# Head projection weights split one projection ahead, and the final norm's products divided by rows between GpSimd and VectorE

## The chip, the core and the metric

The kernel runs on one core of one Trainium2 chip. The metric is device time in microseconds (us). A core has TensorE (PE, the matrix engine, with its weight loads listed as PEld), VectorE (DVE), ScalarE (ACT), GpSimd (POOL) and SyncE (SP), which here only issues DMA transfers. Each engine works through its own queue in order; an instruction whose operand is not ready holds all that stand behind it on that engine. Engines wait for each other by semaphores.

## What is computed

Three different transformer blocks run one after the other on one sequence of 512 tokens with 1024 features, all in float32. The change touches the end of block 1 and the middle of block 3. Block 1 ends with its residual sum and a final norm, and block 2 begins with a norm of its own:

```python
x = x + g2 * expert_choice_ffn(hx2, w_router[l], w_gate[l], w_up[l], w_down[l])
return rms_norm(x, norm_final)          # block 1
...
h = rmsnorm(x, pre_mix_g)               # block 2, first line
```

Block 3 has a mixer with two branches that start from one product of the normed input with `w_in`: latent attention with 8 heads, and a convolution over 31 tokens with a layer norm behind it. Cut to what the change touches:

```python
c_q, c_kv, k_r, u_glu, gate_logits = jnp.split(h @ w_in, IN_OFFSETS, axis=-1)
q = (rms_norm_3(c_q, q_norm) @ w_uq)    # 8 heads x (128 nope + 64 rope columns)
k_nope = rms_norm_3(c_kv, kv_norm) @ w_uk    # 8 heads x 128
scores = q_nope @ k_nope + rope(q_rope) @ rope(k_r)     # then causal softmax, @ v
u = layer_norm(conv31(u_a * sigmoid(u_b)))   # then silu, @ w_pw2
```

## The kernel before

A float32 product is done as three products of two halves: an operand `a` is split into `ah` (a rounded copy, cast by ScalarE at L470) and `al` (the rest, `a - ah`, by VectorE or GpSimd at L471), and TensorE sums `ah*bh`, `ah*bl` and `al*bh` into one PSUM bank. Both operands are split, weights too: `w` gives `wh` and `wl`.

The code is written as generators, one for each strand of work. `run` takes a step of the strand whose made-up clock is behind the others; the numbers in `yield` are what a step is supposed to last. That and a scheduler of the framework fix the order of every engine's queue when the program is built; nothing is decided on the chip.

Head stage of block 3. Five strands run together. `fill3` gives TensorE the bulk of its work: first the rest of the products of `w_in` with the normed input (tiles h3h, h3l, results pj and then gt), then, as soon as the convolution's result uh is there, the 8 blocks of `w_pw3` with it (uhh, uhl). `conv_ln` does the last convolution rows on VectorE (L2207, cv), sums columns on TensorE (cs), subtracts the mean (L2414), squares on ScalarE (L2419, ucq), sums again, scales (L2430, L2438), and ends with a tanh (th), a product on VectorE (L2441, uc) and the split into uhh (ScalarE, L2443) and uhl (GpSimd, L2444). `projs` makes the heads' operands by `proj`, and `heads` does the attention of two heads at a time in `head_pair`: scores (at), softmax on VectorE and ScalarE (mx, prob), transposes of the probabilities on TensorE (pT, copied as probT), and products with v (ao).

`proj(hd)` loads, for every even head, the weights of two heads from `w_uq` into one tile wq (384 columns for the rope parts of both, then 384 for each nope part), makes qr (rope part of the pair), qn (nope part of the head) and kn (from the tile wm, `w_uk`). Each of these three projections goes through `small`: split the weight into wsh and wsl, yield 1600, then 9 products (6 for kn) into the bank sp. The text calls them r1, n2, k2 and so on: r with the number of the pair, n and k with that of the head. There are 4 + 8 + 8 = 20 such splits. The weights of `w_in`, `w_pw3` and so on (tile w) are split on ScalarE and GpSimd. All loads and stores of this stage, wq, w and the stores of gt to memory, stand in SP's one queue; the tiles wq, wm and w share four buffers.

End of block 1. `fin_row(t)` takes the four 128-token rows t = 0 to 3 as four strands. For each it adds the last expert's output to the residual (L1346), multiplies its two halves j = 0, 1 of 512 columns by the gain (L1421, tile y), sums the squares of x and of y on ScalarE (L646, junk), raises to the power -0.5 on GpSimd (L605), scales (L1438, xs) and transposes on TensorE for block 2 (L675, tr, and the split h2h, h2l). The products of L1421 run on VectorE for j = 0 and on GpSimd for j = 1.

Of the kernel before, what the change touches and what calls it, by code (L numbers as in the profile page):

```python
# [11 lines left out]
F32 = mybir.dt.float32  # L12
# [4 lines left out]
OP = mybir.AluOpType  # L17
# [296 lines left out]
def kernel(ctx: ExitStack, tc: tile.TileContext, A, out):  # L314
    nc = tc.nc
    V, P, SC, PE = nc.vector, nc.gpsimd, nc.scalar, nc.tensor

    glob = ctx.enter_context(tc.tile_pool(name="glob", bufs=1))
    wraw = ctx.enter_context(tc.tile_pool(name="wraw", bufs=4))
# [4 lines left out]
    def T(name, dt=F32, n=512):  # L324
        return heap.tile([128, n], dt, name=name, tag="t")
# [6 lines left out]
    def SM(name, n, dt=F32):  # L332
        assert n <= 32
        return glob.tile([128, n], dt, name=name, tag="sm", bufs=24)

    def PS(name="ps"):
        return psum.tile([128, 512], F32, name=name, tag="ps")
# [27 lines left out]
    def tok(t):  # L365
        return slice(128 * t, 128 * t + 128)
# [100 lines left out]
    def split(src, name, w=512, eng=None):  # L467
        hi = T(name + "h", F32R, w)
        lo = T(name + "l", F32R, w)
        SC.copy(hi, src)  # L470
        (eng or V).tensor_tensor(lo, src, hi.bitcast(F32), op=OP.subtract)  # L471
        return hi, lo

    def flat(name, sizes, unit=None):

        off = 0
        for n in sizes:
            yield (A[name][off:off + 128 * n].rearrange("(p c) -> p c", p=128), n,
                   None if unit is None else [unit] * (n // unit), name, None)
            off += 128 * n  # L480
# [35 lines left out]
    for g in G3:  # L516
        n = (b + g + 1) // 2 - (b + 1) // 2
# [3 lines left out]
    ws = Stream(main, [4, 4])  # L521
# [7 lines left out]
    def mm3(ps, a, b, start, stop):  # L529
        mm(ps, a[0], b[0], start, False)  # L530
        mm(ps, a[0], b[1], False, False)
        mm(ps, a[1], b[0], False, stop)
# [71 lines left out]
    def pow_half(y, m, n):  # L604
        P.tensor_tensor(y, m, mhalf[:, :n], op=OP.pow)  # L605
# [28 lines left out]
    def rows_b(name, o=0, w=512):  # L634

        a = T(name)
        src = A["rows"]
        nc.sync.dma_start(a[:, :w], bass.AP(tensor=src.tensor, offset=src.offset + _ROFF[name] + o,
                                            ap=[[0, 128], [1, w]]))
        return a  # L640

    def mean_sq(row):

        ss = SM("ss", 2)
        for j in range(2):
            SC.activation(junk, row[j], AF.Square, scale=1.0 / 32, accum_out=ss[:, j:j + 1])  # L646
        return ss

    def rstd(ss, eps=EPS):
        m = SM("m", 1)  # L650
        V.scalar_tensor_tensor(m, ss[:, 0:1], eps, ss[:, 1:2], op0=OP.add, op1=OP.add)  # L651
        r = SM("r", 1)
        pow_half(r, m, 1)
        return r
# [15 lines left out]
    def turn(t, xs, h):  # L670

        for j in range(2):
            ps = PS("tr")
            for c in range(4):
                PE.transpose(ps[:, tok(c)], xs[j][:, tok(c)], ident)  # L675
            hk, lk = h.h[j][:, :, tok(t)], h.l[j][:, :, tok(t)]
            SC.copy(hk, v4(ps))  # L677
            yield 800
            V.tensor_tensor(lk, v4(ps), hk.bitcast(F32), op=OP.subtract)  # L679
        yield 800  # L680
# [7 lines left out]
    def load_rows(ap, nt, name):  # L688
        r = []
        for t in range(nt):  # L690
            r.append([T(name), T(name)])
            for j in range(2):
                nc.sync.dma_start(r[t][j], ap[tok(t), 512 * j:512 * j + 512])
        return r
# [89 lines left out]
    for k in range(KD):  # L784
# [4 lines left out]
        h, l = hx(k)  # L789
# [101 lines left out]
    for o in range(0, _NM, 512):  # L891
        a = T("mf")
        w = min(512, _NM - o)
# [257 lines left out]
    x1 = load_rows(A["x"], TT, "x1")  # L1151
# [187 lines left out]
    def combine_row(e, t):  # L1339
        ygh, ygl = yg[e]  # L1340
        for d in range(2):
            pc = PS("pc")
            r = slice(64 * d, 64 * d + 64)
            mm(pc, sct[e][r, tok(t)], ygh[r], True, False)
            mm(pc, sct[e][r, tok(t)], ygl[r], False, True)
            V.tensor_tensor(x1[t][d], x1[t][d], pc, op=OP.add)  # L1346
# [6 lines left out]
    for e in range(NE):  # L1353
        hT = [None, None]
        if e == NE - 1:
            ws.caps = [4, 4]
            nf = [rows_b("norm_final", 512 * j) for j in range(2)]
# [29 lines left out]
        for q in range(8):  # L1387
            w, rel = ws.raw()
            for kk in range(2):
                f = 2 * q + kk  # L1390
                p, c, j = f // 8, (f // 4) % 2, f % 4
# [9 lines left out]
        a = T("yg")  # L1401
# [11 lines left out]
    def fin_row(t):  # L1413

        yield 1000 * t
        combine_row(NE - 1, t)
        yield 1500
        y = []
        for j in range(2):
            a = T("y")  # L1420
            (P if j else V).tensor_tensor(a, x1[t][j], nf[j], op=OP.mult)  # L1421
            y.append(a)
        ss = mean_sq(x1[t])
        yield 1700
        r = rstd(ss)
        s2 = mean_sq(y)
        yield 1500
        m, q, r2 = SM("m", 1), SM("q", 1), SM("r2", 1)
        V.tensor_tensor(m, s2[:, 0:1], s2[:, 1:2], op=OP.add)
        V.tensor_tensor(q, r, r, op=OP.mult)  # L1430
        V.tensor_scalar(m, m, q, EPS, op0=OP.mult, op1=OP.add)
        pow_half(r2, m, 1)
        V.tensor_tensor(r2, r2, r, op=OP.mult)
        yield 1200
        xs = []
        for j in range(2):
            a = T("xs")
            V.scalar_tensor_tensor(a, y[j], r2, gm[j], op0=OP.mult, op1=OP.mult)  # L1438
            xs.append(a)
            yield 700  # L1440
        xbs[t] = y, r
        yield from turn(t, xs, h2)
        turned.add(t)
# [98 lines left out]

    proj2 = Persist(dense_t(ws, range(11), h2, use_rw, lead=LD[0]))
    run(*[fin_row(t) for t in range(TT)], proj2.steps(LD[0], lambda: len(turned) > 1))
    del x1, nf, gm
    table("sigmoid_and_others")
# [7 lines left out]
    src = A["rows"]  # L1554
# [719 lines left out]
    cq, ck = pair(cqp), pair(ckp)  # L2274

    def rope(a, dst):
        pr = PS("rot")
        mm(pr, con("rot"), a, True, True)
        b = T("ropeb")
        P.tensor_tensor(dst, a, rope_t[1], op=OP.mult)  # L2280
        V.tensor_tensor(b, pr, rope_t[0], op=OP.mult)
        P.tensor_tensor(dst, dst, b, op=OP.add)
# [5 lines left out]
    uk = list(flat("w_uk3", [2048], 256))  # L2288
    uq = list(flat("w_uq3", [1152] * 4, 384))
    mla_specs += uk + uq  # L2290
    ml = {}
# [9 lines left out]
    def mla_pre():  # L2301

        while 5 not in lat:
            yield 1000
        mla_loads()
        yield from latent_norm([lat[3], lat[4]], 256, "kv_norm_3", "ckn", ckp)
        yield from latent_norm([lat[0], lat[1], lat[2]], 384, "q_norm_3", "cqn", cqp)
        kr = lat[5]
        rope(kr, kr)
        yield 4000  # L2310
        us = []
        for j in range(4):
            us.append(split(ml["uv"][:, 512 * j:512 * j + 512], "wv"))
            yield 1300
        for j in range(2):
            for t in range(TT):
                ps = PS("v3")
                for k in range(2):
                    mm3(ps, ck(k, tok(t)), us[2 * j + k], k == 0, k == 1)
                SC.copy(v3[t][j], ps)  # L2320
                yield 1300
        del ml["uv"]
        for hd in range(2):
            yield from proj(hd)

    def small(src, kd, h):
        u = split(src, "ws", 128 * kd)
        yield 1600
        ps = PS("sp")
        for k in range(kd):  # L2330
            mm3(ps, (u[0][:, tok(k)], u[1][:, tok(k)]), h(k), k == 0, k == kd - 1)
        return ps

    def proj(hd):
        p, h = divmod(hd, 2)
        if h == 0:
            w = wraw.tile([128, 2048], F32, name="wq", tag="w")
            nc.sync.dma_start(w[:, :1152], uq[p][0])
            ml["q"] = w
            yield 4000  # L2340
            qr = T("qr")
            SC.copy(qr, (yield from small(w[:, :384], 3, cq)))
            yield 2500
            ql = T("qro")
            rope(qr, ql)
            ml["qr"] = ql
            yield 2000
        qn = T("qn")
        SC.copy(qn, (yield from small(ml["q"][:, 384 + 384 * h:768 + 384 * h], 3, cq)))
        yield 2500  # L2350
        kn = T("kn3")
        V.tensor_copy(kn, (yield from small(ml["uk"][:, 256 * hd:256 * hd + 256], 2, ck)))
        yield 2000
        qk[hd] = qn, kn, ml["qr"]

# [25 lines left out]
    def projs():  # L2381
        while not pre.over:
            yield 500
        for hd in range(2, 8):
            while hd > done[0] + 3:
                yield 1000
            yield from proj(hd)
# [144 lines left out]
```

## Time and profile before

| | us |
|---|---|
| median of 3 runs | 3052.68 (3047.94 to 3056.89) |
| the profiled execution | 3049.72 |
| its span in the trace | 3047.9 |
| TensorE busy in it | 2790.1 (92%) |
| VectorE busy | 1278.3 (42%) |
| ScalarE busy | 788.0 (26%) |
| GpSimd busy | 463.0 (15%) |

Block 1's mixer and experts last to about 1400 us of the span, block 2 from there to about 2170, block 3 from there to the end; the head stage of block 3 lies between about 2355 and 2595. A line of the timeline gives start and duration in us, engine, line, operation, output and inputs, shape and count; in brackets stands the idle time of the engine just before, and what ended it. Products on TensorE overlap, so their spacing is read from the starts.

### The profile page before, as it was taken

The numbers are of one execution on the slowest core, as the hardware profiler recorded it, in microseconds if no ns is written. First come the engines' busy times: TensorE is split into PE (matmuls) and PEld (weight loads), VectorE is DVE, ScalarE is ACT, GpSimd is POOL, SyncE is SP. The second block draws the span as 40 slices with busy tenths as digits, with TensorE's granted clock in tenths as the row PEclk, the third lists the DMA queues.
The fourth block names the chain that finished last, engine by engine and source line by source line (L and its number), as shares of the span: only waits on it lengthen the run. The fifth ranks groups of instructions, "written<-read, shape, count | busy, mean of one in ns | idle before, by whom it ended". The sixth has DMA issues, their size and how long they took to land.

```text
span 3047.9 us, 34789 instructions
## 1 busy us (share of the span) xinstructions
PE 2790.1 (92%) x13924; PEld 1865.3 (61%) x13924; DVE 1278.3 (42%) x2362; ACT 788.0 (26%) x1629; POOL 463.0 (15%) x438
## 2 busy tenths in 40 slices
PE   6989879898899898886998999999998989999999
PEld 4866564242233232224776788888886756788887
DVE  4157652112111111114377753333699654543334
ACT  3233220000000000004233333223433343442322
POOL 1034230000000000001320111010254332210100
PEclk8999989999999999998999999999999999999999
DMA  6233547999999999996110222222322212422221
GB/s 265 69 118 119 200 172 289 425 425 425 425 425 425 425 426 425 425 423 246 56 42 1 74 93 97 104 83 104 115 97 98 74 60 99 150 84 105 103 90 62
DMA packets 83041, 605.25 MB, mean 199 GB/s; under 512 B 9216, under 2 KB 9472, under 8 KB 29376
## 3 DMA queue, kind: packets, MB, share of 16 engines
q1 hardware_dynamic: 82800, 602.78, 50.0%
q8 instruction: 109, 1.79, 0.2%
q14 instruction: 52, 0.43, 0.0%
q0 software_dynamic: 80, 0.26, 0.0%
HBM read 592.52 MB, written 10.49 MB: 198 GB/s over the span
## 4 chain that ended last, share of the span: by engine, by line
PE 65%; DMA 18%; DVE 12%; ACT 2%; issue 2%; POOL 1%; SPq 0%; DVEq 0%; POOLq 0%; ACTq 0%
PE pj L527 25%; PE pn L527 15%; PE pg L527 9%; DMA wb<-in_w_down_dram 5%; DMA wb<-in_w_gate_dram 4%; DMA wb<-in_w_up_dram 4%; DVE cv L2207 3%; PE py L527 3%; DMA w<-in_w_up_dram 2%; PE pc L527 2%; PE xs L527 1%; PE sp L527 1%; PE at L527 1%; DMA w<-in_w_gate_dram 1%; DMA w<-in_w_down_dram 1%
## 5 line engine op out<-in xcount | busy, mean ns | idle before, releaser
L471 DVE TENSOR_TENSOR wl<-w,wh 128x512 fp32r<-128x512 f32 (+1 forms) x416 | 293.8, 749 | 210.9 <-ACT wh L470 160.1
L527 PE MATMUL pg<-wb,xs 128*64 128x512 f32 x1216 | 287.8, 617 | 51.8 <-DMA wb<-in_w_up_dram 28.0
L470 ACT CAST wh<-w 128x512 fp32r<-128x512 f32 (+1 forms) x510 | 288.5, 617 | 99.2 <-PE pn L527 92.3
L527 PEld LDWEIGHTS pg<-wb,xs 128*64 128x64 f32 x1216 | 87.0, 141 | 228.9 <-issue 155.9
L605 POOL TENSOR_TENSOR r<-m,mhalf 128x1 f32<-128x1 f32 x46 | 30.8, 672 | 1191.1 <-DVE m L651 1185.6
L527 PE MATMUL pg<-w,xs 128*64 128x512 f32 x800 | 188.3, 602 | 5.6 <-DMA w<-in_w_up_dram 3.5
L527 PE MATMUL py<-wb,hidT 128*64 128x512 f32 x584 | 138.8, 622 | 37.9 <-DMA wb<-in_w_down_dram 37.9
L527 PE MATMUL pn<-wh,fh 128*128 128x512 f32 x432 | 168.1, 389 | 0.0
L527 PE MATMUL pn<-wh,fl 128*128 128x512 f32 x432 | 168.1, 389 | 0.0
L527 PE MATMUL pn<-wl,fh 128*128 128x512 f32 x432 | 168.1, 389 | 0.0
L2207 DVE SCALAR_TENSOR_TENSOR cv<-glua,vecs,cv 128x486 f32<-128x486 f32 (+27 forms) x232 | 165.3, 735 | 4.7
L471 POOL TENSOR_TENSOR wl<-w,wh 128x512 fp32r<-128x512 f32 x94 | 124.5, 1344 | 151.1 <-ACT wh L470 114.8
L527 PE MATMUL pj<-h2fh,wh 128*128 128x512 f32 (+1 forms) x376 | 141.3, 378 | 2.5 <-ACT h2fh L677 2.5
L527 PE MATMUL pj<-h2fl,wh 128*128 128x512 f32 (+1 forms) x376 | 141.8, 377 | 0.2 <-DVE h2fl L679 0.2
L527 PE MATMUL pj<-h2fh,wl 128*128 128x512 f32 (+1 forms) x376 | 141.8, 377 | 0.0
L527 PE MATMUL pj<-h3h,wh 128*128 128x512 f32 (+1 forms) x336 | 128.1, 381 | 0.9 <-ACT h3h L677 0.9
L527 PE MATMUL pj<-h3l,wh 128*128 128x512 f32 (+1 forms) x336 | 125.9, 375 | 0.5 <-DVE h3l L679 0.5
L527 PE MATMUL pj<-h3h,wl 128*128 128x512 f32 (+1 forms) x336 | 125.7, 374 | 0.0
L527 PEld LDWEIGHTS pg<-w,xs 128*64 128x64 f32 x800 | 54.5, 137 | 116.1 <-issue 91.0
L1402 DVE SCALAR_TENSOR_TENSOR yg<-py,gsl,g2h 128x512 f32<-128x512 f32 x16 | 12.0, 750 | 261.3 <-PE py L527 261.3
L527 PEld LDWEIGHTS py<-wb,hidT 128*64 128x64 f32 x584 | 43.6, 142 | 127.4 <-issue 97.7
L1334 ACT COPY hidT<-hT 128x512 f32<-128x512 f32 x32 | 18.8, 586 | 393.4 <-PE hT L1332 393.4
(613 smaller groups left out, 5675.2 us busy)
## 6 DMA issues: line engine op xcount, KB each, us to landing
wb<-in_w_gate_dram SPq DMA_DIRECT2D x40, 2048.0 KB, 20.4
wb<-in_w_down_dram SPq DMA_DIRECT2D x36, 2048.0 KB, 20.8
wb<-in_w_up_dram SPq DMA_DIRECT2D x36, 2048.0 KB, 19.7
w<-in_w_down_dram SPq DMA_DIRECT2D x54, 1024.0 KB, 20.4
w<-in_w_up_dram SPq DMA_DIRECT2D x52, 1024.0 KB, 20.0
w<-in_w_gate_dram SPq DMA_DIRECT2D x48, 1024.0 KB, 22.1
w<-in_w_in_dram SPq DMA_DIRECT2D x35, 1024.0 KB, 5.0
w<-in_w_ff_dram SPq DMA_DIRECT2D x30, 1024.0 KB, 4.8
```

The source lines that it names most:

```text
L470: SC.copy(hi, src)
L471: (eng or V).tensor_tensor(lo, src, hi.bitcast(F32), op=OP.subtract)
L527: PE.matmul(ps, a, b, start=start, stop=stop, **kw)
L605: P.tensor_tensor(y, m, mhalf[:, :n], op=OP.pow)
L1334: SC.copy(h, pt)
L1402: V.scalar_tensor_tensor(a, py, gsl[:, e:e + 1], g2h, op0=OP.mult, op1=OP.mult)
L2207: V.scalar_tensor_tensor(acc[:, sh:], a[:, :512 - sh], w[j], acc[:, sh:], op0=OP.mult, op1=OP.add)
```

## The change

`small` no longer splits its own weight at the spot. A weight can be split by `cut` beforehand, and each call of `small` issues, ahead of its own pause and products, the split of the weight that comes next (`nxt`): r names n, n names k, and k of an even head names n of the odd head; k of an odd head names none, so that r and the next pair's n are split when r's turn comes. The load of wq for the next pair moves from the beginning of that pair to the place behind the last nope part of this pair, and the pause of 4000 after it stays for the first pair alone. In `fin_row`, L1421 now runs on GpSimd for both halves of rows 0 and 1 and on VectorE for both halves of rows 2 and 3.

```diff
@@ fin_row
-            (P if j else V).tensor_tensor(a, x1[t][j], nf[j], op=OP.mult)
+            (P if t < 2 else V).tensor_tensor(a, x1[t][j], nf[j], op=OP.mult)
@@
-    def small(src, kd, h):
-        u = split(src, "ws", 128 * kd)
+    cuts = {}
+    def cut(hd, nm):
+        src, kd = {"r": (lambda: ml["q"][:, :384], 3), "n": (lambda: ml["q"][:, 384 + 384 * (hd % 2):768 + 384 * (hd % 2)], 3),
+                   "k": (lambda: ml["uk"][:, 256 * hd:256 * hd + 256], 2)}[nm]
+        cuts[hd, nm] = split(src(), "ws", 128 * kd), kd
+    def small(hd, nm, nxt, h):
+        if (hd, nm) not in cuts:
+            cut(hd, nm)
+            yield 1600
+        if nxt is not None:
+            cut(*nxt)
         yield 1600
+        u, kd = cuts.pop((hd, nm))
         ps = PS("sp")
...
+    def load_q(p):
+        w = wraw.tile([128, 2048], F32, name="wq", tag="w")
+        nc.sync.dma_start(w[:, :1152], uq[p][0])
+        ml["q"] = w
     def proj(hd):
         p, h = divmod(hd, 2)
         if h == 0:
-            w = wraw.tile([128, 2048], F32, name="wq", tag="w")
-            nc.sync.dma_start(w[:, :1152], uq[p][0])
-            ml["q"] = w
-            yield 4000
+            if p == 0:
+                load_q(0)
+                yield 4000
...
-        SC.copy(qn, (yield from small(ml["q"][:, 384 + 384 * h:768 + 384 * h], 3, cq)))
+        SC.copy(qn, (yield from small(hd, "n", (hd, "k"), cq)))
+        if h and hd < 7:
+            load_q(p + 1)
         yield 2500
         kn = T("kn3")
-        V.tensor_copy(kn, (yield from small(ml["uk"][:, 256 * hd:256 * hd + 256], 2, ck)))
+        V.tensor_copy(kn, (yield from small(hd, "k", None if h else (hd + 1, "n"), ck)))
```

Three places where this moves instructions. The first is VectorE during the softmax of head pair 0, where the split of n2 (wsl from wq) stands. Before:

```order
L2414 TENSOR_TENSOR uc<-uc,cb 128x512 x2
L2281 TENSOR_TENSOR ropeb<-rot,sinB 128x512
L1830 RECIPROCAL mx<-mx 128x1 x2
L1831 TENSOR_SCALAR prob<-prob,mx 128x512 x2
L471 TENSOR_TENSOR wsl<-wq,wsh 128x384
L1854 COPY probT<-pT 128x512
```

Now (lines behind the diff are 20 higher, so L2210 keeps its number and L2411 is L2431):

```order
L1831 TENSOR_SCALAR prob<-prob,mx 128x128
L471 TENSOR_TENSOR wsl<-wq,wsh 128x384
L2210 SCALAR_TENSOR_TENSOR uc<-glua,vecs,cv 128x512
L1831 TENSOR_SCALAR prob<-prob,mx 128x128
L1830 RECIPROCAL mx<-mx 128x1
L1831 TENSOR_SCALAR prob<-prob,mx 128x256
L2431 TENSOR_SCALAR mu<-cs_15311 128x4
```

The split went from behind the last scaled probabilities of the pair to ahead of the last convolution row (L2210).

The second is the end of the convolution's layer norm, while the softmax of head pair 1 runs, on VectorE. There wq is split for the nope parts of pair 2 and wm for k4. Before:

```order
L2281 TENSOR_TENSOR ropeb<-rot,sinB 128x512
L2441 SCALAR_TENSOR_TENSOR uc<-th,uc 128x512
L1830 RECIPROCAL mx<-mx 128x1
L1831 TENSOR_SCALAR prob<-prob,mx 128x512
L2441 SCALAR_TENSOR_TENSOR uc<-th,uc 128x512
L471 TENSOR_TENSOR wsl<-wq,wsh 128x384
L1854 COPY probT<-pT 128x512
```

Now:

```order
L1831 TENSOR_SCALAR prob<-prob,mx 128x512
L471 TENSOR_TENSOR wsl<-wm,wsh 128x256
L1830 RECIPROCAL mx<-mx 128x1
L1831 TENSOR_SCALAR prob<-prob,mx 128x512
L2461 SCALAR_TENSOR_TENSOR uc<-th,uc 128x512 x3
L471 TENSOR_TENSOR wsl<-wq,wsh 128x384
L1854 COPY probT<-pT 128x512
```

The split behind the last uc was n4's and is now n5's; n4's stands further up, and k4's ahead of the second 128x512 probability; three uc stand behind that probability instead of one. On ScalarE the same place reads, before:

```order
L470 CAST wsh<-wq 128x384
L2443 CAST uhh<-uc 128x512
L2349 COPY qn<-sp 128x512
L470 CAST wh<-w 128x512 x5
L1854 COPY probT<-pT 128x512
```

Now:

```order
L470 CAST wsh<-wq 128x384
L2463 CAST uhh<-uc 128x512
L1854 COPY probT<-pT 128x512
L470 CAST wh<-w 128x512 x5
L1854 COPY probT<-pT 128x384
```

The copy qn of n4's products went further up, and the casts of the five next weight units now stand behind the first copy of transposed probabilities instead of qn.

The third is GpSimd at the end of block 1 (x_2890 and x_2891 are the halves of row 0, x_2894 and x_2895 of row 1, x_2899 and x_2903 second halves of rows 2 and 3):

```order
 L605 TENSOR_TENSOR r<-m,mhalf 128x1
+L1421 TENSOR_TENSOR y<-x_2890,norm_final 128x512
 L1421 TENSOR_TENSOR y<-x_2891,norm_final 128x512
+L1421 TENSOR_TENSOR y<-x_2894,norm_final 128x512
 L1421 TENSOR_TENSOR y<-x_2895,norm_final 128x512
-L1421 TENSOR_TENSOR y<-x_2899,norm_final 128x512
-L1421 TENSOR_TENSOR y<-x_2903,norm_final 128x512
 L605 TENSOR_TENSOR r<-m,mhalf 128x1
```

GpSimd keeps four products at the same place in its queue, between the power for row 0 and the next one; VectorE takes the four of rows 2 and 3 instead of the first halves, with one small operation (L651) in their middle instead of behind them.

On SP the loads of wq after the first are issued earlier: the second keeps its place but for one swap of a store with a load, the third moves ahead of the first two loads of `w_pw3`, the fourth ahead of the last.

## Rows read from the trace of the kernel before

**Rows 1.** The page: busy time, share of the span, instructions of TensorE and others.

```profile
PE 2790.1 (92%) x13924; PEld 1865.3 (61%) x13924; DVE 1278.3 (42%) x2362; ACT 788.0 (26%) x1629; POOL 463.0 (15%) x438
```

**Rows 2.** TensorE's waits, 2355 to 2575 us: us in total, times, longest.

```profile
PE sp L527 <- ACT wsh L470: 12.5, 5, 6.7
PE sp L527 <- DVE wsl L471: 5.5, 2, 3.1
```

**Rows 3.** Timeline of TensorE in the head stage, rows with idle time ahead.

```profile
2397.37 0.50 PE L527 MATMUL sp<-cknh,wsh 128*128 128x512 f32 x1 [0.98 <-ACT wsh L470]
...
2431.49 0.50 PE L527 MATMUL sp<-cqnh,wsl 128*128 128x512 f32 x1 [3.10 <-DVE wsl L471]
...
2485.51 0.79 PE L527 MATMUL sp<-cqnh,wsh 128*128 128x512 f32 x1 [6.68 <-ACT wsh L470]
...
2493.62 0.79 PE L527 MATMUL pj<-uhh,wh 128*128 128x512 f32 x1 [1.19 <-ACT wh L470]
...
2517.81 0.50 PE L527 MATMUL sp<-cknh,wsh 128*128 128x512 f32 x1 [1.07 <-ACT wsh L470]
...
2588.81 1.98 PE L527 MATMUL ao<-probT,v 128*128 128x512 f32 x4 [0.77 <-ACT probT L1854]
```

**Rows 4.** Busy time by windows: stretch, length, each engine, clock, DMA.

```profile
2440.00:2464.00 24.00, 24.00 (x123) 17.84 (x121) 12.16 (x24) 7.62 (x17) 2.29 (x2) 1.00 0.25 85
2464.00:2494.00 30.00, 16.55 (x51) 8.49 (x51) 23.32 (x54) 16.58 (x39) 14.12 (x11) 0.83 0.01 5
```

**Rows 5.** Timeline of TensorE after its waits: the spacing of products.

```profile
2432.54 0.57 PE L527 MATMUL sp<-cqnh,wsh 128*128 128x512 f32 x1
...
2435.90 0.45 PE L527 MATMUL pj<-h3h,wh 128*128 128x512 f32 x1
...
2494.98 0.80 PE L527 MATMUL pj<-uhh,wl 128*128 128x512 f32 x1
...
2497.59 0.39 PE L527 MATMUL pj<-uhh,wl 128*128 128x512 f32 x1
2497.82 0.40 PE L527 MATMUL pj<-uhh,wh 128*128 128x512 f32 x1
...
2498.52 1.58 PE L1852 MATMUL pT<-cons,prob 128*128 128x128 f32 x13
```

**Rows 6.** Timelines of VectorE, ScalarE and GpSimd where uh is finished.

```profile
2485.73 1.75 DVE L2441 SCALAR_TENSOR_TENSOR uc<-th,uc 128x512 f32<-128x512 f32 x1
2487.41 1.61 DVE L471 TENSOR_TENSOR wsl<-wq,wsh 128x384 fp32r<-128x384 f32 x1
...
2487.52 0.62 ACT L2443 CAST uhh<-uc 128x512 fp32r<-128x512 f32 x1 [2.06 <-DVE uc L2441]
...
2485.49 4.67 POOL L2444 TENSOR_TENSOR uhl<-uc,uhh 128x512 fp32r<-128x512 f32 x3
2493.65 6.22 POOL L471 TENSOR_TENSOR wl<-w,wh 128x512 fp32r<-128x512 f32 x5 [3.49 <-ACT wh L470]
```

**Rows 7.** Timelines of VectorE (splits of r0, r1 and r2) and SP (second wq).

```profile
2368.28 0.76 DVE L471 TENSOR_TENSOR wsl<-wq,wsh 128x384 fp32r<-128x384 f32 x1 [4.33 <-ACT wsh L470]
...
2411.42 1.64 DVE L471 TENSOR_TENSOR wsl<-wq,wsh 128x384 fp32r<-128x384 f32 x1
...
2473.36 0.55 DVE L471 TENSOR_TENSOR wsl<-wq,wsh 128x384 fp32r<-128x384 f32 x1
...
2391.93 0.33 SPq L2338 DMA_DIRECT2D wq<-in_w_uq_dram  x1
```

**Rows 8.** Timelines of VectorE, GpSimd and TensorE at the final norm.

```profile
1407.73 4.63 DVE L1421 TENSOR_TENSOR y<-x,norm_final 128x512 f32<-128x512 f32 x4
1413.42 0.15 DVE L1429 TENSOR_TENSOR m<-ss 128x1 f32<-128x1 f32 x1
...
1408.79 5.91 POOL L1421 TENSOR_TENSOR y<-x,norm_final 128x512 f32<-128x512 f32 x4
...
1416.76 1.97 PE L675 MATMUL tr<-cons,xs 128*128 128x128 f32 x8 [12.77 <-DVE xs L1438]
```

More of the change, by code (lines that the diff above doesn't have):

```diff
@@ L2336, in proj @@
         if h == 0:
-            w = wraw.tile([128, 2048], F32, name="wq", tag="w")
-            nc.sync.dma_start(w[:, :1152], uq[p][0])
-            ml["q"] = w
-            yield 4000
+            if p == 0:
+                load_q(0)
+                yield 4000
             qr = T("qr")
-            SC.copy(qr, (yield from small(w[:, :384], 3, cq)))
+            SC.copy(qr, (yield from small(hd, "r", (hd, "n"), cq)))
             yield 2500
```

## The prediction

> **What bounds the kernel now.** I read the page first: TensorE is busy for 92% of the span [rows 1]. Such a kernel gains from an edit only where TensorE stands still, so the next view is the list of TensorE's waits in the stretch of the head projections, 2355 to 2575 us, and then its timeline there for the place of each. The reader is to see three things.
>
> First, 12.5 + 5.5 = 18.0 us of those waits are for the two halves of a projection weight (wsh from ScalarE, wsl from VectorE) [rows 2]. Second, they lie in three places of different kind [rows 3]. In head pair 0 it is 0.98 and 3.10 us, with products over h3 still to be done behind them. In pair 1 the h3 products are used up: from 2464 to 2494 TensorE is busy for 16.55 of 30 us and VectorE for 23.32 [rows 4], so VectorE paces that stretch, with the softmax of pair 1 and the end of the convolution's layer norm, which makes the operand uh. In pairs 2 and 3 it is 1.07 us each (one row stands for both), with uh products around them. Third, after a wait products start 0.42 us apart instead of 0.23 us [rows 5]; the clock of 0.83 from 2464 to 2494 mixes the two levels of 1.2 and 2.4 GHz [rows 4].
>
> At the other place of the change, the end of block 1, TensorE stands still for 12.77 us [rows 8]: there the latency of the final norm is the path.
>
> **The change part by part.** No instruction is added or removed: 20 splits, four loads of wq and eight products of the final norm before and after. All is order.
>
> *Pair 0.* The split of head 2's nope weight (n2) stood on VectorE behind both scaled 128x512 probabilities; now it stands ahead of the last convolution row. With the halves there, TensorE runs on into h3 products that it has in its queue anyway: 0.98 + 3.10 = 4.1 us gained. After the 3.10 us, eight products start in the 3.36 us from 2432.54 to 2435.90 [rows 5]; at 0.23 us they take 1.8, so 1.5 us more. The cover is the h3 work; were it gone, the wait would return as one for the convolution. What comes next is fed by TensorE: the column sums of the layer norm stand in its queue, and VectorE is busy for only 12.16 of the 24 us from 2440 to 2464 [rows 4], so the earlier arrival is passed on.
>
> *Pair 1.* TensorE stands still for 30 - 16.55 = 13.4 us, but this cannot all go: the products over uh need the last uhh and uhl, and VectorE's chain up to there is nearly the same. So I cost it from the end of that chain. The last uc ends at 2485.73 + 1.75 = 2487.48 [rows 6]. Then followed the split of n4 (1.61 us), nine products at half pace, the copy qn, only then the five casts of the next stage's weights, and GpSimd's first half of them: the third product over uh, the first that needs that half, starts at 2494.98 [rows 5], 7.5 us after the last uc. Now there follow the last uhh (0.62), a probT copy whose transposes are done, and the casts; GpSimd has to finish one uhl (4.67 / 3 = 1.56) and one wl (6.22 / 5 = 1.24) [rows 6]. With two hand-overs of about 0.1 (an estimate) that is 3.6 us: 3.9 us gained. Against it, the splits of n4 and k4 now stand ahead of the second 128x512 probability, so in the chain: 0.55 each where GpSimd stands still, 1.64 at worst [rows 7]. I take 1.1 for both (0.55 is the row of this stretch), with 3.3 as the bound. Eight transposes move from after the first uh products into TensorE's idle time, 1.58 / 13 = 0.12 each [rows 5]: 0.9 us gained.
>
> The longer rest is paid in clock. Before, TensorE restarted at 2485.51 [rows 3] and was back to 0.23 us at 2497.59 [rows 5], 12.1 us later. Now it restarts with the eight transposes, about 1.7 us before the last uc ends (the operation ahead of that uc), so 5.3 us before the third uh product; if the return takes 12.1 us again, 6.8 us run at half pace there and lose 3.4, where the 2.6 us from 2494.98 to 2497.59 lose 1.3. So +2.1 us, bounds 0 and +4. Sum for pair 1: -3.9 + 1.1 - 0.9 + 2.1 = -1.6 us out of 13.4.
>
> One price weighed: a split took 0.55 us on VectorE with GpSimd idle, and 1.61 and 1.64 us while GpSimd ran a subtract [rows 6, 7]. By the Trainium skill ("SBUF — State Buffer", SBUF: two separate sides) a VectorE operation with two SBUF inputs and a GpSimd operation take their shared ports as a lock, and the loser stands still for the whole instruction. The trace agrees in these rows. By it, the two moved splits could each meet a GpSimd subtract, and this part would be 2.2 us worse.
>
> *Pairs 2 and 3, and the end.* 1.07 + 1.07 = 2.1 us gained. In the last pair 12 products over uh now stand between the transposes and the first ao product, 2.7 us of cover for a wait of 0.77 [rows 3]: 0.8 us gained.
>
> *The loads.* Each wq load after the first is issued one projection earlier; on SP's queue the second still has two weight loads and four stores of gt between the first and itself, the third now goes ahead of the first two loads of the pw weights and the fourth ahead of the last. The second was issued at 2391.93 [rows 7], 5.4 us before the k1 products, which still come ahead of pair 0's softmax [rows 3]. ScalarE's cast of its rope part now stands ahead of that softmax, so a landing later than that would hold ScalarE: nothing, bound +3 (the worst wait of pair 0). The pw weights are wanted only at 2493.62 [rows 3]: nothing.
>
> *The final norm.* Row 0's two products are now both on GpSimd, whose first starts at 1408.79 as before, since the power for row 0 stands ahead of it. Four products last 5.91 us there and four 4.63 us on VectorE, as many on each as before [rows 8]. At 1.48 us each, row 0's second is ready at 1411.7 rather than 1410.3. The VectorE operation that wants its sum of squares stands behind VectorE's four products and one small one and started at 1413.42, 1.7 us after that; the power that it feeds waits for GpSimd's four products to 1414.7 in both orders. So the 12.77 us stay: 0, bounds -1.5 and +1.5 (one GpSimd product either way in ScalarE's queue of squares).
>
> *Sum.* -4.1 - 1.5 - 1.6 - 2.1 - 0.8 + 0 = -10.1 us. The profiled execution took 3049.72 us (span 3047.9 and 1.8 around it): 3039.6. It was 3.0 us under the median of the runs, 3052.68, so on the median 3042.6.
>
> **The rivals.**
> *Pair 0's gain turns into another wait.* TensorE arrives earlier at the convolution's column sums and waits there for VectorE: the 4.1 and 1.5 us go, and -4.5 us remain: 3048.2. For it: VectorE paces everything that ends in uh. Against it: the list has no wait of TensorE for a convolution row, and VectorE has idle time between the two norms [rows 2, 4].
>
> *GpSimd in the way.* Both moved splits meet a GpSimd subtract: 2.2 us worse, 3044.8. For it: 1.61 and 1.64 us; against: GpSimd is busy for only 14.12 of those 30 us [rows 4]. This is what the Trainium skill's rule above would make of it.
>
> *The kernel gets slower.* A split issued earlier is also a VectorE instruction that waits for ScalarE's cast while softmax and convolution stand behind it. A wait of that kind of 4.33 us is in the trace [rows 7]. Five splits (r1, n2, r2, n4, k4) move ahead of work that leads to uh; at 4.33 us each the chain grows by 21.7, net +11.6: 3064.3. It decides from 2.0 us for each split. For it: VectorE and ScalarE work in order. Against it: in the new order each cast stands ahead of softmax pieces that it used to wait behind, so its other half should find it done.
>
> *More than I count.* The clock costs nothing more (2.1) and the chain to uh is 3 us shorter, since k3's products come sooner after the column sums: 3037.5.
>
> That the change does not do what it says holds for the rope weight alone: it is still split on the spot, but with the nope weight's split and two pauses ahead of its products; the sum has it so.
>
> **How the numbers follow.** Forecast (3038 to 3048) 0.50; pair 0 handed on 0.18; GpSimd in the way 0.10; more 0.10; slower 0.12. A measurement of this kernel tells about 0.3% (9.2 us) from no change, so faster means under 3043.5: 0.30 from the forecast, 0.10 from "more", 0.05 from the third case, 0.45. Slower means over 3061.9: 0.12. Within: 0.43. Range: 3035, the gain without the clock's price and with the best bounds, to 3056, which leaves out the slower case and little more.
>
> **What will show it.** Right: the waits for wsh and wsl are gone or under 2 us in all; in pair 1 TensorE waits for the scaled 128x512 probability, not for a split; the third uh product starts some 4 us after the last uc; the idle time ahead of the first transpose of the final norm is 12.77 us within 1.5. Wrong: VectorE's waits for wsh over 2 us each, a wait for a convolution row, ScalarE waiting for wq's load, or a longer rest at the final norm.

## The result and the profile after

The changed kernel takes 3039.41 us (median of 4 runs, 3037.10 to 3040.82); the kernel before, run beside it, 3054.78 us. The ratio is 0.9946, with a 95% interval of 0.993 to 0.9961: 12 to 21 us faster, 15.4 us between the medians. 3042.6 us with a range of 3035 to 3056 were predicted. The sign and the place were right and the idle time was nearly so; the clock was mis-sized, and the experiments show that the prediction's reason (weights split ahead) is only one of two edits in the change that each bring all of the gain or nearly all. The gain is half as large again as the 10.1 us of the sum. That the time still lies only 3.2 us from the forecast is in part luck: the forecast starts from a median of 3052.68 us, 2.1 below that of the kernel before as it ran beside the changed one.

TensorE's instructions are the same in number; this is the page's line to be held against [rows 1]:

```profile
PE 2797.0 (92%) x13924; PEld 1868.2 (61%) x13924; DVE 1278.8 (42%) x2362; ACT 788.2 (26%) x1629; POOL 463.3 (15%) x438
```

TensorE's waits in the changed kernel, 2355 to 2580 us (total, times, longest):

```profile
PE pj L527 <- ACT wh L470: 4.3, 1, 4.3
PE pT L1852 <- DVE prob L1831: 3.0, 2, 1.7
PE pT L1852 <- DVE mx L1822: 2.6, 1, 2.6
PE pj L527 <- POOL wl L471: 1.0, 1, 1.0
PE at L527 <- DVE kn L2372: 0.2, 1, 0.2
```

The 18.0 us of waits for wsh and wsl of [rows 2] are gone to the last one. In their place stand 5.6 us for the softmax of pair 1 and 5.3 us for the halves of the *next* stage's weights (`w_pw3`, w_pw in the profile).

To compare executions, the head stage needs two marks that stand in every trace: the start of the last value product (v) and that of the first product over ath, the operand of the stage behind the heads. Before and after:

```profile
2363.00 0.39 PE L527 MATMUL v<-wvh,cknl 128*128 128x512 f32 x1
...
2593.81 0.48 PE L527 MATMUL pj<-ath,wh 128*128 128x512 f32 x1
```

```profile
2369.64 0.39 PE L527 MATMUL v<-wvh,cknl 128*128 128x512 f32 x1
...
2480.81 0.33 PE L1852 MATMUL pT<-cons,prob 128*128 128x128 f32 x1 [2.65 <-DVE mx L1822]
2482.81 0.87 PE L1852 MATMUL pT<-cons,prob 128*128 128x128 f32 x2 [1.68 <-DVE prob L1831]
2484.96 0.47 PE L1852 MATMUL pT<-cons,prob 128*128 128x128 f32 x1 [1.27 <-DVE prob L1831]
2489.75 0.79 PE L527 MATMUL pj<-uhh,wh 128*128 128x512 f32 x1 [4.32 <-ACT wh L470]
...
2492.01 0.80 PE L527 MATMUL pj<-uhh,wl 128*128 128x512 f32 x1 [1.04 <-POOL wl L471]
...
2495.16 0.42 PE L527 MATMUL pj<-uhh,wh 128*128 128x512 f32 x1
...
2586.43 0.47 PE L527 MATMUL pj<-ath,wh 128*128 128x512 f32 x1
```

The stage fell from 2593.81 - 2363.00 = 230.8 us to 216.8: 14.0 us. Adding up the bracketed idle times of TensorE between the marks gives 20.3 us before and 11.2 after; that is 9.1 of the 14.0, and the other 4.9 lie in the pace of the products. The spans of these two profiled executions differ by only 8.8 us, because the one after was slower ahead of the marks, by lower clock in places that the change does not touch (last section). That is why single profiles are compared between the marks, and kernels by their medians.

### The profile page after: what moved, and what is told of

Same layout as the page of the kernel before. It is cut to its first block, busy times and chain, and to the rows that moved or that the text cites. A ratio compares the mean times of both kernels' runs of the same rounds, so it can differ in the third digit from the quotient of the medians.

```text
span 3039.1 us, 34792 instructions
## 1 busy us (share of the span) xinstructions
PE 2797.0 (92%) x13924; PEld 1868.2 (61%) x13924; DVE 1278.8 (42%) x2362; ACT 788.2 (26%) x1629; POOL 463.3 (15%) x438
## 4 chain that ended last, share of the span: by engine, by line
PE 67%; DMA 16%; DVE 12%; ACT 2%; POOL 2%; issue 2%; SPq 0%; POOLq 0%; DVEq 0%; ACTq 0%
PE pj L527 25%; PE pn L527 15%; PE pg L527 9%; DMA wb<-in_w_down_dram 5%; DMA wb<-in_w_up_dram 3%; PE py L527 3%; DVE cv L2207 3%; DMA wb<-in_w_gate_dram 3%; PE pc L527 2%; DMA w<-in_w_up_dram 2%; PE xs L527 1%; PE sp L527 1%; PE at L527 1%; DMA w<-in_w_gate_dram 1%; DMA w<-in_w_down_dram 1%
```

## The experiments

All kernels of this section, with the head stage between the marks and TensorE's idle time in it (worked out from each timeline as above), and the time as a ratio to the kernel before:

| kernel | head stage, us | idle, us | ratio of times (95%) |
|---|---|---|---|
| before | 230.8 | 20.3 | 1 |
| changed | 216.8 | 11.2 | 0.9946 (0.993 to 0.9961) |
| e1, norm by rows alone | 230.5 | 20.2 | 0.999 (0.998 to 1.0) |
| e2, head projections alone | 217.8 | 11.0 | 0.9948 (0.9935 to 0.996) |
| e3, order alone (load, pause) | 216.5 | 10.9 | 0.9941 (0.9927 to 0.9954) |
| e4, splits ahead alone | 218.0 | 12.1 | 0.9963 (0.9951 to 0.9976) |
| e5, load alone | 232.0 | 20.3 | 0.9996 (0.9986 to 1.0007) |
| e8, pause alone | 217.5 | 10.8 | 0.9941 (0.9929 to 0.9953) |
| e6, changed + early w_pw splits | 212.5 | 6.2 | 0.9934 (0.992 to 0.9947) |
| e7, e6 + norm rows swapped | 212.5 | 6.4 | 0.9922 (0.9909 to 0.9936) |
| e9, e8 + early w_pw splits | 218.9 | 11.8 | 0.9967 (0.9957 to 0.9978) |
| e10, e6 + a value split on GpSimd | 212.5 | 6.4 | 0.9925 (0.9909 to 0.994) |

The first four kernels took the change apart. My theory was that splitting ahead makes the gain.

**The two halves of the change.** e1 is the kernel before with the norm's line, e2 the changed kernel without it.

```diff
-            (P if j else V).tensor_tensor(a, x1[t][j], nf[j], op=OP.mult)
+            (P if t < 2 else V).tensor_tensor(a, x1[t][j], nf[j], op=OP.mult)
```

> The kernel before with only the final norm's change: its products by rows (both of rows 0 and 1 on GpSimd, both of rows 2 and 3 on VectorE). My theory (the gain of about 15 us is made in the head stage of block 3 and the norm gives nothing, because the first transpose after it still waits 12.8 us): 0 us, within 1.5 us either way, and the same wait of 12.8 us ahead of the first transpose. Rival A (the norm's change carries part of the gain): 3 to 8 us faster, with a shorter wait there. Rival B (it costs something later in block 2, where the trace of the changed kernel shows a stretch of TensorE at the lower clock near 1731 us that the trace of before does not have): 3 to 4 us slower, with that stretch at the lower clock in this kernel's trace too.

> The changed kernel with the final norm's products by halves as before, so that only the head projections' change is left. My theory: all of the gain, 13 to 16 us faster than before. Rival A (the norm carries part): 8 to 12 us faster. Rival B (the norm's change costs 3 to 4 us in block 2): 17 to 19 us faster.

e1 took 3050.85 us against 3054.22, a difference at the edge of its interval; its head stage and its wait at the norm (12.84 us) are those of before. e2 took 3036.84, 15.9 us less by its ratio. So the head projections make the gain. e1's interval alone would leave rival A up to 6 us, but the shorter wait that it needs is not there, and e2 keeps the whole gain without the norm's edit. Rival B does not hold: the stretch of lower clock near 1731 us is in neither kernel's trace (clock 1.00 from 1730 to 1736 us in both), and in e9 below it comes without the norm's edit (last section).

**The head projections' change, in two.** e3 has the load of wq one projection earlier and no pause at the heads of pairs 1 to 3, but each split at its use (against the changed kernel; the norm's line is as before in e3 and e4):

```diff
-        if (hd, nm) not in cuts:
-            cut(hd, nm)
-            yield 1600
-        if nxt is not None:
-            cut(*nxt)
+        cut(hd, nm)
         yield 1600
```

> Of the head projections' change only the order: the load of a pair's weights behind the n products of the pair before, and no pause of 4000 planned ns at the head of pairs 1 to 3; each split is still made when its own projection asks for it. The final norm as before. My theory (the gain comes from the splits standing a projection ahead, so that their casts and subtractions lie behind other products): the waits for split weights stay, 10 to 18 us of them between 2355 and 2575 us, and the time is within 3 us of before. Rival (the gain comes from the projections being taken up earlier, which brings pair 1's scores and TensorE's filling products closer together): 8 us faster or more, with the waits for split weights still there in part.

e4 has the splits ahead, but load and pause as before:

```diff
         if h == 0:
-            if p == 0:
-                load_q(0)
-                yield 4000
+            load_q(p)
+            yield 4000
...
-        if h and hd < 7:
-            load_q(p + 1)
```

> Of the head projections' change only the splits one projection ahead; the load of a pair's weights and the pause of 4000 planned ns stand at the head of each pair as before. The final norm as before. My theory: the waits for split weights go (under 3 us of them left between 2355 and 2575 us) and the time is 8 to 15 us below before. Rival (earlier projections bring it): within 4 us of before, though the waits for split weights are gone, since a wait for the scaled scores or for the convolution's last outputs takes their place.

e4 came out as my theory says: no wait for a split head weight is left, and 11.3 us are gained (0.37% of 3054), 12.8 between the marks. But e3 gained 18.0 us with every split at its use, where the theory allowed 3. The theory falls as a statement on what is needed: splitting ahead is sufficient for nearly all of the gain, and so is something in the order.

**Load or pause.** e5 is the kernel before with the earlier load alone; e8 the kernel before without the pause:

```diff
             ml["q"] = w
-            yield 4000
+            if p == 0:
+                yield 4000
             qr = T("qr")
```

> The kernel before with one line moved: the load of a pair's projection weights stands behind the n products of the pair before, as in the changed kernel; the pause of 4000 planned ns stays at the head of every pair, and the splits are made at their use. TensorE's order is that of before. Theory now (the pause's removal made the gain of the kernel with load and pause changed, since the weights had landed long before their split in before too): 0 us, within 2 us. Rival (the earlier load made it): 12 to 18 us faster.

> The kernel before with one edit: no pause of 4000 planned ns at the head of pairs 1 to 3. The load stays at the head of its pair, the splits at their use; TensorE's order is that of the kernel with load and pause changed. Theory now (the pause): 14 to 18 us faster than before, with the 3.1 us wait for split weights in pair 0's stretch gone. Rival (the earlier load was needed): under 6 us faster, with ScalarE or VectorE waiting for the weights' load ahead of a split.

The load brings nothing (0.9996), the pause's removal everything (0.9941, as e3). Here is how one deleted number does the work of the splits. Pair 0's wait of 3.10 us [rows 3] was for n2's low half, which stood on VectorE behind the scaling of the last softmax rows, and those lasted 3.02 us, with GpSimd at work beside them from 2426.92 on (the kernel before, VectorE):

```profile
2426.88 3.02 DVE L1831 TENSOR_SCALAR prob<-prob,mx 128x512 f32<-128x512 f32 x2
2429.83 1.61 DVE L471 TENSOR_TENSOR wsl<-wq,wsh 128x384 fp32r<-128x384 f32 x1
```

Without the pause, pair 1's projections are taken up earlier, and the same split lands ahead of those rows (which take 0.88 us there; GpSimd's next work starts at 2429.74, in their middle). In e8, VectorE and then TensorE:

```profile
2424.25 0.72 DVE L471 TENSOR_TENSOR wsl<-wq,wsh 128x384 fp32r<-128x384 f32 x1
...
2429.32 0.88 DVE L1831 TENSOR_SCALAR prob<-prob,mx 128x512 f32<-128x512 f32 x2
```

```profile
2426.27 0.39 PE L527 MATMUL sp<-cqnh,wsh 128*128 128x512 f32 x1
```

The split is over at 2424.97, its first product starts at 2426.27 with nothing to wait for. What e8 still waits for, 2355 to 2580 us:

```profile
PE sp L527 <- ACT wsh L470: 8.7, 3, 6.5
PE sp L527 <- DVE wsl L471: 1.0, 2, 0.8
PE pj L527 <- POOL wl L471: 0.6, 1, 0.6
PE at L527 <- DVE kn L2353: 0.6, 1, 0.6
```

So e8 keeps 9.7 us of waits for split weights and is as fast as the changed kernel, which has none. In pair 1 the name on the wait does not matter: TensorE idles there for 13.3 us before, 11.2 in the changed kernel, 9.3 in e8 and 8.8 in e4 (for w_pw's wh, 7.1 us, wl, 1.0, and one score, 0.7).

**What ends pair 1's idle time in the changed kernel.** ScalarE, VectorE and GpSimd there:

```profile
2488.08 0.62 ACT L2463 CAST uhh<-uc 128x512 fp32r<-128x512 f32 x1 [0.47 <-DVE uc L2461]
2488.60 0.58 ACT L1854 COPY probT<-pT 128x512 f32<-128x512 f32 x1
2489.08 2.70 ACT L470 CAST wh<-w 128x512 fp32r<-128x512 f32 x5
...
2486.72 1.32 DVE L2461 SCALAR_TENSOR_TENSOR uc<-th,uc 128x512 f32<-128x512 f32 x1 [0.61 <-ACT th L624]
2487.96 1.62 DVE L471 TENSOR_TENSOR wsl<-wq,wsh 128x384 fp32r<-128x384 f32 x1
...
2486.23 4.50 POOL L2464 TENSOR_TENSOR uhl<-uc,uhh 128x512 fp32r<-128x512 f32 x3 [1.61 <-ACT uhh L2463]
2490.68 2.50 POOL L471 TENSOR_TENSOR wl<-w,wh 128x512 fp32r<-128x512 f32 x2
```

w_pw's first cast starts at 2489.08, behind the eighth uhh and one copy of probT, and its subtraction at 2490.68, right behind the eighth uhl. They did not wait for data. SP's queue and the transfers of the same kernel (issue, then KB each and median us to landing):

```profile
2440.89 2.57 SPq L417 DMA_DIRECT2D w<-in_w_pw_dram  x2
...
w<-in_w_pw_dram SPq DMA_DIRECT2D x3, 1024.0 KB, 4.7
```

By these the weights had landed some 40 us before they were cast (2440.89 + 2.57 + 4.7 = 2448.2, an estimate from the median). `fill3` asks for the first split only when all of uh is written. The Trainium skill ("PSUM — Partial Sum Buffer", Engine vs sequencer instructions) calls the queues of these three engines strict FIFO; the rows agree. e6 makes the first four of these splits ahead of that point:

```diff
         ws.open()
+        yield 5000
+        for n in range(1, 5):
+            ws.fill(n)
+            yield 1300
         while "uh" not in ready:
```

> The changed kernel, with the first four splits of the pointwise convolution's weights (5000 planned ns behind the opening of that stream, one each 1300) made while the convolution's norm still runs, where the changed kernel makes them behind its last output. Theory (what ends the hole of pair 1 in the changed kernel is neither the head weights nor the softmax but ScalarE's casts of these weights, queued behind the eight casts of the norm's outputs, and GpSimd's subtraction behind them): the waits of 4.3 us and 1.0 us ahead of the first pointwise product shrink to under 2 us together, and the time is 3 to 6 us below the changed kernel. Rival (the outputs themselves end last, so TensorE waits for the eighth one's low half on GpSimd instead): within 1.5 us of the changed kernel.

Waits of e6 in the same window:

```profile
PE pT L1852 <- DVE prob L1831: 3.6, 2, 2.7
PE pj L527 <- POOL uhl L2464: 2.0, 2, 1.1
PE pj L527 <- ACT uhh L2463: 0.4, 1, 0.4
PE at L527 <- DVE kn L2372: 0.2, 1, 0.2
```

The waits for wh and wl are gone, 2.4 us for uhh and uhl have come, and the head stage is 212.5 us, 4.3 less than in the changed kernel and 5.3 less than in e2. Theory and rival each had a part: the casts ended last, and behind them the outputs themselves. In times it is 0.9934 against 0.9946, the right size, though the intervals overlap.

**What the splits ahead are worth then.** e9 adds the same early w_pw splits to e8, which splits its head weights at their use.

> The kernel without the pause (the only edit of that run: no pause of 4000 planned ns at the head of pairs 1 to 3, splits at their use), and beside it the first four splits of the pointwise weights made early, as in the run that added them to the changed kernel. It tells what the splits one projection ahead are worth once the pause is gone. Theory (without splits ahead TensorE still stands 6.5 us at pair 2's k weights, in front of the pointwise products, so their early splits cannot be used): within 2 us of the kernel without the pause, and 3 to 5 us of idle time of TensorE more than with the splits ahead, measured from the last value product to the first product of the next stage (10 to 11 us of idle time there, against 6.2 us with splits ahead). Rival (the early pointwise splits alone bring it): idle time there of 6 to 7 us, 4 us below the kernel without the pause.

Its waits for split weights, 2355 to 2580 us:

```profile
PE sp L527 <- ACT wsh L470: 10.8, 4, 7.6
PE sp L527 <- DVE wsl L471: 1.1, 2, 0.9
```

The kind of thing expected came: TensorE stands 7.6 us at pair 2's k weights, in front of the w_pw products that could now run; there are 11.8 us of idle time (10 to 11 were expected) against 6.2 in e6, and a head stage 6.4 us longer. So splitting ahead adds nothing to the missing pause as long as w_pw's casts come late anyway, and 6.4 us once they come early. One thing did not come out: e9's time was to be within 2 us of e8's, and its ratio, 0.9967, lies 0.26% above (8 us), while its head stage is only 1.5 us longer. The profiled executions, 7.2 us apart in span, show where the rest went in them: ahead of the first mark, in two stretches of the last section that the edit does not touch. From the same product to the same product it is 7.40 us in e9 and 4.26 in e8 near 1730 us, and 37.7 against 33.4 at the value products. Whether the other runs differ for the same reason no trace shows; the two ran on different chips.

**The final norm, the other way round.** e7 is e6 with rows 0 and 1 on VectorE:

```diff
-            (P if t < 2 else V).tensor_tensor(a, x1[t][j], nf[j], op=OP.mult)
+            (V if t < 2 else P).tensor_tensor(a, x1[t][j], nf[j], op=OP.mult)
```

> The kernel of the run with the early pointwise splits, and beside it the final norm's rows the other way round: rows 0 and 1 on VectorE (0.6 us a product), rows 2 and 3 on GpSimd (1.5 us). Theory (row 0's two products stand on the path to the first transpose, and GpSimd makes the second of them 1.7 us after VectorE would): the wait ahead of the first transpose falls from 12.8 us by 0.8 to 1.5 us, the time by as much. Rival (rows 2 and 3 on GpSimd end later than their squares need them, and their transposes wait): the first wait falls, a later one grows, and the time is within 0.5 us of the run without the swap.

The theory was wrong; the first wait grew. e7's first transpose, and GpSimd and VectorE ahead of it:

```profile
1416.69 1.54 PE L675 MATMUL tr<-cons,xs 128*128 128x128 f32 x6 [13.12 <-DVE xs L1438]
...
1412.15 0.55 POOL L605 TENSOR_TENSOR r<-m,mhalf 128x1 f32<-128x1 f32 x1 [0.76 <-DVE q L1430]
1412.67 2.48 POOL L1421 TENSOR_TENSOR y<-x,norm_final 128x512 f32<-128x512 f32 x2
1415.12 1.06 POOL L605 TENSOR_TENSOR r<-m,mhalf 128x1 f32<-128x1 f32 x2
...
1415.69 0.16 DVE L1433 TENSOR_TENSOR r<-r,r 128x1 f32<-128x1 f32 x1 [3.23 <-POOL r L605]
```

Row 0's sums are there early, but the power that they feed stands on GpSimd behind two products (1412.67 to 1415.15), and VectorE waits 3.23 us for it. The transpose starts 15.51 us after the first of the expert's combining products (pc) instead of 15.22 in e6. The time (0.9922 against 0.9934) cannot tell 0.3 us.

**The value weights.** e10 is e6 with one of four value splits on GpSimd:

```diff
-            us.append(split(ml["uv"][:, 512 * j:512 * j + 512], "wv"))
+            us.append(split(ml["uv"][:, 512 * j:512 * j + 512], "wv", eng=P if j == 1 else None))
```

> The changed kernel with the early pointwise splits, and beside it the second of the four value-weight splits subtracted on GpSimd instead of VectorE, where it stood behind five of the convolution's taps. Theory (the stretch ahead of the head stage, 33.4, 35.0 or 37.5 us from the first rotation product to the last value product in the profiles so far, is longer where TensorE waits 3.2 us for that subtraction and then works at the lower clock): no wait over 1 us at the value products, 31 to 32 us for that stretch, and 2 to 5 us less in time. Rival (VectorE's next subtraction or GpSimd's queue ends last there instead): that stretch stays at 33 us or more and the time within 1.5 us of the run without this edit.

The only wait at the value products is now 0.75 us, and the stretch from the first rotation product to the last value product is 31.7 us, as expected. In time it is 0.9925 against e6's 0.9934: 2.7 us, inside what was expected, but the intervals overlap. e7 and e10 had the shortest times (3031.94 and 3029.79 us, against 3057.20 and 3055.46 before), 6 to 7 us under the changed kernel by the ratios to before; what the traces show of that is the 4.3 to 5.3 us of the w_pw splits and, for e10, the value products' stretch.

## Why the prediction came out as it did

Between the marks the prediction's sum is -10.1 us and the profiles give -14.0. Its steps:

*Pair 0.* The waits of 0.98 and 3.10 us are gone, as said, and no wait for the column sums took their place: the rival in which pair 0's gain is handed on does not hold. The last uc ends 118.4 us behind the first mark (2486.72 + 1.32 - 2369.64), before 124.5 [rows 6]. That is 6.1 us gained; the terms for pair 0 (5.6) and for the two splits in the chain (+1.1) make 4.5. The 1.6 us more were gained in pair 0: VectorE's first operation behind the second column sums (cm) starts 86.5 us behind the first mark before (2449.47) and 79.2 now (2448.81), 7.3 us earlier. From there to the last uc 1.2 us are lost again, near the 1.1 charged. k4's split lasted 0.41 us, n4's 0.55 at 2468.29, with GpSimd idle; but VectorE also waits 2.77 us there for TensorE's products cb, where it did not wait before, and the two causes were not told apart.

*Pair 1, from the last uc to the third uh product.* 3.6 us predicted, 2492.01 - 2488.04 = 3.97 measured, before 7.5. The order of events is the predicted one, down to the eighth uhl and the one wl on GpSimd. What I read as the pace of VectorE's chain had a second limit behind it, w_pw's casts on ScalarE; the sum had their position, and did not see that they could have stood 40 us earlier. So only half of the sign given for pair 1 held: TensorE waits there for the softmax, as said, but its longest wait, 4.32 us, is for a split after all, one of w_pw.

*The clock: the step that failed.* I took 12.1 us from restart to full pace from [rows 3, 5], put the restart 5.3 us ahead of the third uh product, and charged +2.1 us. In the changed kernel the eight transposes are done 2.6 us before the last uc ends (2484.96 + 0.47, against 2488.04), the third uh product starts at 2492.01, and products start 0.23 to 0.25 us apart from 2495.16 on. From the third uh product on, 3.15 us at half pace lose 1.6 us, where the prediction had 3.4 and the kernel before lost 1.3: +0.3 instead of +2.1. The 12.1 us had further waits in them (2.35 us and the 1.19 of [rows 3]). The slow stretch itself did not get shorter; by windows, before and after:

```profile
2484.00:2497.00 13.00, 7.95 (x17) 5.01 (x18) 4.99 (x5) 5.21 (x10) 9.51 (x7) 0.50 0.00 0
```

```profile
2482.00:2495.00 13.00, 5.56 (x12) 3.46 (x13) 7.53 (x11) 7.92 (x15) 10.23 (x8) 0.50 0.24 82
```

The granted clock is 0.50 (1.2 GHz) for these 13 us in both, but TensorE is busy for 7.95 of them before and for 5.56 now: more of the slow stretch falls into idle time. And products that used to run at half pace behind their own waits no longer do: the 72 products of the n and r weights with a low half in them took 19.1 us from start to next start before (idle time left out) and 16.4 after; all 156 products of the head projections took 40.4 and 36.8. Together TensorE's pace gave back 4.9 us, where the sum had +0.6 (-1.5 and +2.1): 5.5 better. Idle time fell by 9.1, where the sum's terms for it make 10.7 (4.1, pair 1's 3.7, 2.1 and 0.8): 1.6 worse, all of it in pair 1, whose idle time fell by 2.1. The two make the difference of 3.9. "The clock costs nothing more" was a rival at 0.10, with a shorter chain; that case is nearest to what happened.

*Pairs 2 and 3, the end.* All three waits are gone, 2.9 us, as summed.

*The loads.* Nothing, as said: e5 is the test.

*The final norm.* Nothing, as said, and for the reason given, GpSimd's queue ahead of the power. After:

```profile
1417.20 1.11 PE L675 MATMUL tr<-cons,xs 128*128 128x128 f32 x4 [12.83 <-DVE xs L1438]
...
1409.17 5.98 POOL L1421 TENSOR_TENSOR y<-x,norm_final 128x512 f32<-128x512 f32 x4
1415.11 1.58 POOL L605 TENSOR_TENSOR r<-m,mhalf 128x1 f32<-128x1 f32 x3
```

12.83 us against 12.77 [rows 8]. e7 broke on the very point that the prediction had seen.

*GpSimd in the way.* The two splits that were priced took 0.55 and 0.41 us, so neither was held up. n5's split met GpSimd's subtractions (1.62 us, in the rows above, beside 4.50 us of uhl), and it was wanted 14 us later; k2's did too (1.51 us at 2434.68, beside wl; 0.42 to 0.43 elsewhere), five us before its products. The Trainium skill ("SBUF — State Buffer", SBUF: two separate sides), by which one of two such operations stands still, agrees with these rows; the rival it would have made did not happen, because the collisions stood off the path.

*Slower.* It did not happen. VectorE's waits for ScalarE's casts were 12.4 us in four places between 2370 and 2490 us, before 11.4 in four from 2364 to 2500; but the five splits that the rival named (r1, n2, r2, n4, k4) waited for none. The long ones, over the 2 us that the prediction named as a sign of being wrong, were 6.9 us at r0's and n0's and 4.1 at n3's, after which VectorE still waited 5.1 us for TensorE's second column sums. The pace of the convolution was not set there.

The attribution was incomplete: the prediction names the removed pauses only in passing, prices none of them, and gives the gain to the splits. e8 shows that the pause's removal alone would have done it, and e4 that the splits alone would have as well, or nearly.

## What to carry to other kernels

A wait for an operand can be removed by making the operand earlier or by taking up the consumer's strand at another point of the planned order; try the one-number edit alone before crediting the larger one. Where several waits stand in a row in front of the same late operand (here uh), removing one only renames the idle time; look for preparations that sit behind that operand in a queue though their data landed long ago. And an early product is of use only if nothing that still waits stands before it in its engine's queue, so edits that bring nothing one by one can be worth something together.

## What the runs showed of the hardware

After the same wait, in the same instructions, TensorE's clock falls in one execution and stays in another. Near 1730 us, which the change does not touch, the kernel before and the changed one have a wait of 0.97 us each; by windows (length, busy time of PE, PEld, DVE, ACT, POOL, clock, DMA), before and after:

```profile
1725.00:1730.00 5.00, 3.93 (x28) 2.96 (x27) 2.06 (x5) 2.87 (x9) 0.00 (x0) 1.00 0.00 0
1730.00:1736.00 6.00, 5.49 (x48) 4.57 (x49) 3.01 (x9) 2.33 (x7) 1.65 (x1) 1.00 0.00 0
```

```profile
1725.00:1730.00 5.00, 3.93 (x28) 2.96 (x26) 2.77 (x5) 2.87 (x9) 0.00 (x0) 1.00 0.00 0
1730.00:1736.00 6.00, 6.00 (x33) 5.26 (x34) 0.75 (x3) 0.00 (x0) 1.65 (x1) 0.55 0.00 0
```

After the wait TensorE runs at 2.4 GHz in the one and almost all of the window at 1.2 GHz in the other; the product behind the wait starts at 1729.16 and 1729.90, and the same later product at 1733.41 and 1737.26, so the stretch cost 3.1 us. The wait of 0.97 us is in all twelve profiles of this case. In eight of the other ten, e1 and e2 among them, the two products start 4.25 or 4.26 us apart as in the kernel before; in e10 it is 5.87, and in e9 7.40, almost as in the changed kernel:

```profile
1730.00:1736.00 6.00, 5.30 (x29) 4.57 (x30) 0.95 (x4) 0.65 (x2) 1.65 (x1) 0.61 0.00 0
```

Ahead of the head stage, the value products wait for their second low half from VectorE; before and after:

```profile
2342.24 0.50 PE L527 MATMUL v<-wvl,cknh 128*128 128x512 f32 x1 [2.51 <-DVE wvl L471]
```

```profile
2342.16 0.50 PE L527 MATMUL v<-wvl,cknh 128*128 128x512 f32 x1 [0.67 <-DVE wvl L471]
...
2346.30 0.79 PE L527 MATMUL v<-wvl,cknh 128*128 128x512 f32 x1 [3.17 <-DVE wvl L471]
```

Behind the longer wait products start 0.43 us apart (before: 0.23), and the stretch from the first rotation product (rot) to the last value product is 37.6 us instead of 33.4. Over the profiles it was 33.4 (before, e2, e6, e8), 35.0 (e1, e5, e7) or 37.5 to 37.7 (changed, e3, e4, e9) with no regard to which part of the change a kernel has; only e10, which removes the wait, left that set (31.7). The kernel before spread over 16.5 us in 17 runs beside e5 to e8 (3047.81 to 3064.31); an effect of a few us shows in a trace between two marks long before it shows in times.
